# Soft mixture of experts on one core: 21 result tiles at fixed places in turn, instead of at the next free place of a shared pool

## The chip, the cores and the metric

The kernel runs on one core of one Trainium2 chip. The metric is the device time of one execution in microseconds (us). The kernel before takes 1521.05 us, the median of 3 runs (1519.95 to 1521.68).

A core has a matrix engine (PE, with PEld for its weight loads), a vector engine (DVE), a scalar engine (ACT), a GpSimd engine (POOL) and SyncE (SP). In this kernel SP and POOL do almost nothing but issue DMA transfers. Every engine runs its own list of instructions strictly in the order of that list; a wait at the head of a list holds up all that stands behind it.

## The reference

Every token gets all eight experts, weighted by a softmax over its router logits:

```python
probs = softmax(router_logits)                  # 16 x 512 x 8
output = 0                                      # 16 x 512 x 2048
for e in range(8):
    output += probs[:, :, e:e+1] * (x @ expert_weights[e])   # 512 -> 2048
```

Written as one product this is Z times W: Z has 8192 rows (tokens) and 8 x 512 columns (x scaled by each expert's probability), W has 8 x 512 rows and 2048 columns.

## The kernel before

The product is done in a seven-product (Strassen-Winograd) scheme. On the outer level, tokens come in pairs of row blocks of 256, the experts in two groups of four, and the output columns in two halves of 1024. Four of the seven outer products (called 1, 5, 2 and 4) are computed in four stages by `sub_product`, which applies the same scheme once more inside. Their results go to DRAM, to the buffers `kept1`, `kept5`, `kept2` and `kept4`, in tiles of 128 tokens x 512 columns of float32 (256 KB). The remaining three outer products (6, 7 and 3) are computed in the last stage, the loop over `q` at line 432, here called the main stage, and are added there to the kept ones.

`sub_product` (lines 284 to 339) runs over row blocks; for each of two sets of 128 tokens (`u`) it does seven products of 8 matmuls and fills eight result tiles: four copies of a PSUM bank made by ACT (`keep`, line 316) and four sums made by DVE (`put`, line 321), which SP stores to DRAM (`to_kept`).

The main stage has 16 values of `q`, two of `u` and two of `n`: 64 turns, each a column half of 512 columns for one row block pair. Here a turn is called a half and numbered from 0. A half needs four loads by SP of kept products (`from_kept`, line 279), in the order m1, m5, m4, m2, and does this:

1. ACT copies m1 into a PSUM bank (line 461).
2. DVE adds m2 to m1 in m2's tile (line 462, called the m2 sum), and POOL stores it to the output. This needs no result of PE.
3. PE adds 16 matmuls (operand s2) to that bank; DVE adds m5 (line 465, the first sum, into m1's tile).
4. PE adds 16 more (s3) to the same bank, and can begin only when the first sum has read it. DVE makes two sums, into m5's and m4's tiles (lines 467 and 469), and POOL stores both.
5. PE does 16 matmuls (s4) in another bank; DVE adds it to m1's tile (line 471, the last sum), and POOL stores it.

Ahead of this DVE makes the operands a11, s2, s3, s4 for each `u` by four multiplications (`mul`) and three subtractions from xT and pT tiles, which SP loads; there are 8 such tiles (`xpool`).

The order of each engine's list and the place of each tile in SBUF are worked out when the program is built, by a planner that walks the program with costs of its own for each instruction and takes, for each engine, the earliest instruction in program order that it believes to be ready. On the chip the lists and places are fixed, and semaphores hold an instruction until its data and its place are really free.

All result tiles of `sub_product`, all loads of kept products, and the small tiles of the softmax and the identity come from one pool, `hpool`, under one name with 21 places of 2 KB per partition. In the program as built, tiles take these places strictly in program order, each the place that the planner believes to have been free longest. So no load of the main stage gets a place before the last result tile of the fourth stage has got one. In the middle of the main stage m1 and m2 get the place of the tile 26 back, m5 of that 29 back, and m4 of that 3 back, which is m2 of the half before, since m2 is given up early.

The lines that matter below: `softmax` at 152, `early_p` at 195, `early_z` at 202, `half` at 273, `from_kept` at 279, `sub_product` at 284, and the main stage at 432 to 472. L88 is the one line at which every DVE addition, subtraction or multiplication is recorded, L99 that of SP's DMAs, L102 that of POOL's loads, L108 that of the matmuls.

Of the kernel before, what the change touches and what calls it, by code (L numbers as in the profile page):

```python
# [19 lines left out]


# [1 line left out]

# [8 lines left out]
def kernel(  # L32
# [8 lines left out]
    P = 128  # L41
    f16 = mybir.dt.float16
    f32 = mybir.dt.float32
# [4 lines left out]
    E, _, EH = expert_weights.shape  # L48
    T = B * S
    C = H // P  # L50
    HE = E // 2
    NB = 512
# [11 lines left out]
    zpool = ctx.enter_context(tc.tile_pool(name="zpool", bufs=12))  # L64
    xpool = ctx.enter_context(tc.tile_pool(name="xpool", bufs=8))
    spool = ctx.enter_context(tc.tile_pool(name="spool", bufs=5))
    hpool = ctx.enter_context(tc.tile_pool(name="hpool", bufs=21))

# [7 lines left out]

    K8 = 2 * C
    BLOCKS = ((0, 0), (1, 0), (0, 1), (1, 1))  # L80

    last = {}

    def note(i):
        last[i.ins.engine] = i.ins

    def tt(o, a, b, op):
        note(nc.vector.tensor_tensor(out=o, in0=a, in1=b, op=op))  # L88

    @contextmanager  # L90
    def behind():

        with ExitStack() as stack:
            for i in list(last.values()):
                stack.enter_context(tc.issue_after(i))
            yield

    def sp(o, i):
        note(nc.sync.dma_start(out=o, in_=i))  # L99
# [4 lines left out]
    def bank():  # L104
        return psum.tile([P, NB], f32, name="ps", tag="ps")

    def mm(ps, z, w, start, stop):
        nc.tensor.matmul(ps, z, w, start=start, stop=stop, skip_group_check=True)  # L108
# [5 lines left out]
    def new_w():  # L114
        return wpool.tile([P, K8, NB], f16, name="w", tag="w")

    def cast_w(q, kn, e, t):
        k, n = kn
        pool(t[:, ds(e * C, C), :],
             expert_weights[(q // 10 - 1) * HE + 2 * k + e, :,  # L120
                            ds((q % 10 - 1) * NH + n * NB, NB)].rearrange("(c p) n -> p c n", p=P))

    def load(what, kn, gate=True):
        t = new_w()
        if gate:
            note(nc.vector.memset(t.rearrange("p (e c) n -> p e c n", e=2)[:, :, 0, 0:2], 0.0))  # L126
        if (what, kn) in stored:
            pool(t, stored[what, kn])
        else:
            for e in range(2):  # L130
                cast_w(what, kn, e, t)
        return t
# [17 lines left out]


    def softmax(lg, J):
        mx = hpool.tile([P, J], f32, name="mx", tag="h")
        nc.vector.tensor_reduce(out=mx, in_=lg, axis=AX, op=mybir.AluOpType.max)
        tt(lg, lg, mx.unsqueeze(2).to_broadcast([P, J, E]), SUB)
        nc.scalar.activation(out=lg, in_=lg, func=mybir.ActivationFunctionType.Exp)  # L156
        sm = hpool.tile([P, J], f32, name="sm", tag="h")
        nc.vector.tensor_reduce(out=sm, in_=lg, axis=AX, op=ADD)
        nc.vector.reciprocal(out=sm, in_=sm)
        pf = hpool.tile([P, E, J], f32, name="pf", tag="h")  # L160
        tt(pf, lg.rearrange("p j e -> p e j"), sm.unsqueeze(1).to_broadcast([P, E, J]), MUL)
        return pf

# [4 lines left out]
    def cast_x(row):  # L168
        xs = spool.tile([P, H], f16, name="xs", tag="xs")
        pool(xs, x_f[ds(row, P), :])  # L170
        return xs
# [2 lines left out]
    early = [2 * HQ * (j // 2) + P * (j % 2) for j in range(NF)]  # L174
    lg0 = []
    for t in range(2):
        lg0.append(hpool.tile([P, 4, E], f32, name="lg0", tag="h"))
        for j in range(0, 4, 2):
            sp(lg0[t][:, ds(j, 2)], lg_f[ds(early[4 * t + j], 2 * P), :].rearrange("(j p) e -> p j e", p=P))
    xs0 = [cast_x(row) for row in early[:2]]  # L180
    ident = hpool.tile([P, P], f16, name="ident", tag="h")
    nc.vector.memset(ident, 1.0)
    nc.gpsimd.affine_select(out=ident, in_=ident, compare_op=mybir.AluOpType.is_equal, fill=0.0, base=0,
                            pattern=[[-1, P]], channel_multiplier=1)
    xs0 += [cast_x(row) for row in early[2:4]]
    b11 = {kn: new_w() for kn in BLOCKS}
    with behind():
        for kn in BLOCKS[:3]:
            for e in range(2):
                cast_w(11, kn, e, b11[kn])  # L190
    xs0 += [cast_x(row) for row in early[4:]]
    for e in range(2):
        cast_w(11, BLOCKS[3], e, b11[BLOCKS[3]])

    def early_p(t):
        pf = softmax(lg0[t], 4)
        ph = hpool.tile([P, HE, 4], f16, name="ph0", tag="h")
        note(nc.vector.tensor_copy(ph, pf[:, 0:HE]))
        return ph
    ph0 = [early_p(0)]  # L200

    def early_z(j, dest):

        diag = hpool.tile([P, HE, P], f16, name="diag", tag="h")
        tt(diag, ident.unsqueeze(1).to_broadcast([P, HE, P]),
           ph0[j // 4][:, :, ds(j % 4, 1)].to_broadcast([P, HE, P]), MUL)
        for c in range(C):
            ps = bank()
            mm(ps, xs0[j][:, ds(c * P, P)], diag.rearrange("p e t -> p (e t)"), True, True)
            src = ps.rearrange("p (e t) -> p e t", e=HE)  # L210
            for i, o in enumerate(dest(c)):
                note((nc.scalar.copy if c % 2 else nc.vector.tensor_copy)(  # L212
                    o, src if o.shape[1] == HE else src[:, ds(2 * i, 2)]))

    z0 = []
    for j in range(4):
        z = zpool.tile([P, HE, C, P], f16, name="z", tag="z")
        early_z(j, lambda c: [z[:, :, c, :]])
        z0.append(z.rearrange("p e c t -> p (e c) t"))
    ph0.append(early_p(1))  # L220
    z1 = [[zpool.tile([P, 2, C, HQ], f16, name="z", tag="z") for k in range(2)] for t in range(2)]


    R = 4
    J = HQ // R
    p_dram = dram.tile([NHQ, 3 * HE, HQ], f16, name="p_dram")
    lg_v = lg_f.rearrange("(h r j) e -> r h j e", r=R, j=J)
    lg = hpool.tile([P, J, E], f32, name="lg", tag="h")
    for r in range(R):
        sp(lg[ds(r * NHQ, NHQ)], lg_v[r])  # L230
    pf = softmax(lg, J)
    ph = hpool.tile([P, 3 * HE, J], f16, name="ph", tag="h")
    nc.scalar.copy(ph[:, 0:HE], pf[:, HE:E])
    nc.scalar.copy(ph[:, HE:2 * HE], pf[:, 0:HE])
    tt(ph[:, 2 * HE:], pf[:, 0:HE], pf[:, HE:E], ADD)
# [35 lines left out]
    kept = {r: [dram.tile([2, HQ, NB], f32, name=f"kept{r}_{i}") for i in range(NI)] for r in (1, 2, 4, 5)}  # L271

    def half():
        return hpool.tile([P, NB], f32, name="h", tag="h")

    def to_kept(r, i, u, n, t):
        sp(kept[r][i][n, ds(u * P, P), :], t)
# [1 line left out]
    def from_kept(r, i, u, n):  # L279
        t = half()  # L280
        sp(t, kept[r][i][n, ds(u * P, P), :])
        return t

    def sub_product(r, odd, first, w, prep, start=0, zs=None):

        for d in range(start, NI // 2):
# [19 lines left out]
            for u in range(HQ // P):  # L306
                banks = {}

                def prod(p, b, start=True):
                    if start:  # L310
                        banks[b] = bank()
                    for k in range(K8):
                        mm(banks[b], z[p][:, k, ds(u * P, P)], w[p][:, k, :], start and k == 0, k == K8 - 1)
                    return banks[b]

                def keep(ps):
                    t = half()
                    nc.scalar.copy(t, ps)  # L318
                    return t

                def put(t, n, a, b, op):
                    o = half()
                    tt(o, a, b, op)
                    to_kept(r, 2 * d + t, u, n, o)

                r1 = keep(prod(1, "x"))
                put(0, 0, prod(2, "b"), r1, ADD)
                r5 = keep(prod(5, "q"))
                r2 = keep(prod(6, "x", False))
                put(0, 1, prod(3, "q", False), r2, ADD)  # L330
                prod(7, "x", False)
                r3 = keep(banks["x"])
                put(1, 1, banks["x"], r5, ADD)
                put(1, 0, r3, prod(4, "d"), SUB)
# [16 lines left out]
    for n in range(2):  # L351
        ps = [bank() for _ in range(4)]
        for k in range(2):
            for e in range(2):
                for j in range(4):
                    for c in range(C):
                        mm(ps[j], z0[j][:, (2 * k + e) * C + c, :], b11[k, n][:, e * C + c, :],
                           k + e + c == 0, k + e == 2 and c == C - 1)
        for j in range(4):
            o = half()  # L360
            nc.scalar.copy(o, ps[j])  # L361
            to_kept(1, j // 2, j % 2, n, o)
        for j in range(2 * n, 2 * n + 2):
            early_z(4 + j, lambda c: [z1[j // 2][k][:, :, c, ds(j % 2 * P, P)] for k in range(2)])
        if n == 0:
            with behind():
                w = finish(inner_weights(b11, new_w()))


    def weights_of_t1():  # L370
        b = {}
        for i, kn in enumerate(BLOCKS):
            b[kn] = load(12, kn)
# [9 lines left out]
    def weights_of_21():  # L383
        b = {}
        yield
        for kn in BLOCKS:
            b[kn] = load(21, kn)
# [7 lines left out]
    def weights_of_t4():  # L395
        b = {}
        for i, kn in enumerate(BLOCKS):
            t, t2 = load(22, kn), load("t1", kn)
# [103 lines left out]
```

## Time and profile before

| | |
|---|---|
| median of 3 runs | 1521.05 us |
| the profiled execution | 1525.74 us |
| its span, first to last instruction | 1524.0 us |
| PE busy | 1468.5 us, 6712 matmuls |
| DVE busy | 1006.9 us |
| ACT busy | 199.9 us |
| mean granted PE clock | 0.990 |
| DMA | 344.60 MB, mean 226 GB/s |

The profiled execution takes 4.7 us more than the median of the runs. The four stages end at about 794 us of the span and the main stage takes the rest. The page's second part shows the span in 40 slices of 38.1 us, in tenths; before the last slice PE dips only in the 21st to 24th, and its clock only in the 22nd, at the change from the fourth stage to the main one.

### The profile page before, as it was taken

The page shows a single profiled execution, that of the slowest core. Times are in us where ns is not written, and L with a number is a line of the kernel's source. Part 1 is how long each engine was busy: PE and PEld are TensorE (multiplying, and loading weights), DVE is VectorE, ACT ScalarE, POOL GpSimd, SP SyncE. Part 2 cuts the span into 40 slices and gives each one's busy share as a digit, 9 for nine tenths or more (in the row PEclk, how much of TensorE's full clock was granted, in tenths as well). Part 3 has the DMA queues.
Part 4 walks back from the last instruction along what each step waited for, and adds up shares of the span by engine and source line. Part 5 has one row for each costly group of instructions (what it writes and reads, how often), then busy time and mean ns, then how long its engine had stood idle before and what let it go on. Part 6 is the DMA issues. An engine that isn't in the chain of part 4 may idle for free.

```text
span 1524.0 us, 18110 instructions
## 1 busy us (share of the span) xinstructions
PE 1468.5 (96%) x6712; PEld 658.3 (43%) x6712; DVE 1006.9 (66%) x1148; ACT 199.9 (13%) x350; POOL 220.2 (14%) x397
## 2 busy tenths in 40 slices
PE   9999999999999999999987889999999999999997
PEld 3444444444444444444433334444444444444443
DVE  6866776566867868667575656676667666766622
ACT  3211111111111121111110000000000000000000
POOL 3201101110001000010001111212211121212111
PEclk9999999999999999999998999999999999999999
DMA  9999967999579954699659766777777676777521
GB/s 163 236 221 256 238 166 180 235 273 236 170 240 346 345 194 134 180 266 296 250 212 394 232 205 228 239 229 239 230 240 219 227 226 229 232 243 228 201 104 62
DMA packets 200920, 344.60 MB, mean 226 GB/s; under 512 B 55808, under 2 KB 85504, under 8 KB 195200
## 3 DMA queue, kind: packets, MB, share of 16 engines
q1 hardware_dynamic: 145408, 220.75, 47.1%
q0 software_dynamic: 55424, 122.71, 28.8%
q8 instruction: 52, 0.85, 0.2%
q14 instruction: 36, 0.29, 0.1%
HBM read 201.62 MB, written 163.77 MB: 240 GB/s over the span
## 4 chain that ended last, share of the span: by engine, by line
PE 52%; issue 37%; POOL 9%; DMA 2%; POOLq 0%; DVE 0%; ACT 0%; SPq 0%; ACTq 0%; DVEq 0%
PE ps L108 52%; POOL out_dram L457 9%; DMA h<-kept 1%; DMA pT<-p_dram 1%; POOLq L457 0%; DMA lg<-in_router_logits_dram 0%; DVE h L88 0%; DVE z L88 0%; ACT L156 0%; SPq L99 0%; DVE diag L88 0%; ACT ps L461 0%; POOLq L497 0%; ACT lg L156 0%; DVE pf L88 0%
## 5 line engine op out<-in xcount | busy, mean ns | idle before, releaser
L108 PE MATMUL ps<-w,z 128*128 128x512 f16 x6672 | 1455.6, 380 | 42.1 <-DVE h L88 26.3
L108 PEld LDWEIGHTS <-z 128*128 128x128 f16 x6672 | 653.5, 98 | 843.6 <-issue 66.9
L88 DVE TENSOR_TENSOR h<-ps,h 128x512 f32<-128x512 f32 x442 | 298.0, 687 | 321.3 <-PE ps L108 207.5
L88 DVE TENSOR_TENSOR z<-xT,pT 128x2048 f16<-128x2048 f16 x248 | 299.2, 1218 | 21.5 <-PE ps L108 12.2
L88 DVE TENSOR_TENSOR z<-z 128x2048 f16<-128x2048 f16 x220 | 268.5, 1222 | 34.6 <-PE ps L108 25.3
L318 ACT COPY h<-ps 128x512 f32<-128x512 f32 x248 | 145.4, 586 | 601.8 <-PE ps L108 591.8
L457 POOL DMA_DIRECT2D out_dram<-h x256 | 138.4, 541 | 582.5 <-DVE h L88 567.1
L461 ACT COPY ps<-h 128x512 f32<-128x512 f32 x64 | 37.7, 590 | 640.9 <-DVE h L88 607.4
L88 DVE TENSOR_TENSOR h<-h 128x512 f32<-128x512 f32 x64 | 44.2, 690 | 96.4 <-DMA h<-kept 88.0
L102 POOL DMA_DIRECT2D xs<-in_x_dram x72 | 38.6, 539 | 304.3 <-DMA xT<-xs 296.8
L88 DVE TENSOR_TENSOR w<-w 128x4096 f16<-128x4096 f16 x32 | 73.0, 2286 | 4.8 <-PE ps L108 3.1
L88 DVE TENSOR_TENSOR h<-h,ps 128x512 f32<-128x512 f32 x62 | 42.3, 682 | 11.7 <-PE ps L108 11.7
L102 POOL DMA_DIRECT2D w<-in_expert_weights_dram x40 | 30.0, 761 | 134.5 <-DVE w L126 85.8
L102 POOL DMA_DIRECT2D w<-wd x12 | 6.5, 539 | 242.2 <-DVE w L126 135.1
L212 DVE CAST z<-ps 128x256 f16<-128x256 f32 (+1 forms) x24 | 10.7, 506 | 8.8 <-PE ps L108 8.8
L108 PE MATMUL ps<-diag,xs 128*128 128x512 f16 x32 | 10.2, 483 | 2.5 <-DVE diag L88 2.5
L102 POOL DMA_DIRECT2D w<-wdt x12 | 6.5, 546 | 32.0 <-DVE w L88 17.8
L212 ACT CAST z<-ps 128x256 f16<-128x256 f32 (+1 forms) x24 | 9.2, 479 | 4.3 <-PE ps L108 4.2
L108 PEld LDWEIGHTS <-xs 128*128 128x128 f16 x32 | 3.7, 118 | 9.1 <-issue 7.2
L361 ACT COPY h<-ps 128x512 f32<-128x512 f32 x8 | 4.7, 585 | 15.7 <-PE ps L108 15.7
L88 DVE TENSOR_TENSOR diag<-ident,ph 128x512 f16<-128x512 f16 x8 | 5.2, 685 | 0.1
L76 PE MATMUL every<-zero 128*128 128x512 f16 x8 | 3.6, 631 | 1.3 <-DVE zero L73 1.3
(20 smaller groups left out, 13.1 us busy)
## 6 DMA issues: line engine op xcount, KB each, us to landing
kept<-h SPq DMA_DIRECT2D x256, 256.0 KB, 4.8
h<-kept SPq DMA_DIRECT2D x256, 256.0 KB, 3.4
out_dram<-h POOLq DMA_DIRECT2D x256, 256.0 KB, 3.7
pT<-p_dram SPq DMA_DIRECT2D x124, 256.0 KB, 4.8
w<-in_expert_weights_dram POOLq DMA_DIRECT2D x40, 512.0 KB, 12.9
xT<-x SPq DMA_DIRECT2D x60, 256.0 KB, 4.2
wdt<-w SPq DMA_DIRECT2D x12, 1024.0 KB, 8.5
w<-wdt POOLq DMA_DIRECT2D x12, 1024.0 KB, 14.0
```

The source lines that it names most:

```text
L76: nc.tensor.matmul(every[:, i, :], zero[:, 0:P], zero, start=True, stop=True)
L88: note(nc.vector.tensor_tensor(out=o, in0=a, in1=b, op=op))
L102: note(nc.gpsimd.dma_start(out=o, in_=i))
L108: nc.tensor.matmul(ps, z, w, start=start, stop=stop, skip_group_check=True)
L212: note((nc.scalar.copy if c % 2 else nc.vector.tensor_copy)(o, src if o.shape[1] == HE else src[:, ds(2 * i, 2)]))
L318: nc.scalar.copy(t, ps)
L361: nc.scalar.copy(o, ps[j])
L457: nc.gpsimd.dma_start(out=out_f[ds((2 * q + odd) * HQ + u * P, P), ds(cols * NH + n * NB, NB)], in_=t)
L461: nc.scalar.copy(ps, m1)
```

## The change

The pool of 21 shared places becomes 21 names of one place each, h0 to h20. A counter hands the names out in the order in which the program asks for tiles, so a tile always takes the place of the tile asked for 21 before it, whatever the planner believes to be free. Five small tiles that live long or come early (two logit tiles, the identity, two probability tiles) leave the pool for places of their own in a second pool, `cpool`.

```diff
+from itertools import count
...
-    hpool = ctx.enter_context(tc.tile_pool(name="hpool", bufs=21))
+    hpool = ctx.enter_context(tc.tile_pool(name="hpool", bufs=1))
+    cpool = ctx.enter_context(tc.tile_pool(name="cpool", bufs=1))
...
+    turn = count()
+
+    def h_tile(shape, dtype):
+
+        return hpool.tile(shape, dtype, name="h", tag=f"h{next(turn) % 21}")
...
-        mx = hpool.tile([P, J], f32, name="mx", tag="h")
+        mx = h_tile([P, J], f32)
...
-        sm = hpool.tile([P, J], f32, name="sm", tag="h")
+        sm = h_tile([P, J], f32)
...
-        pf = hpool.tile([P, E, J], f32, name="pf", tag="h")
+        pf = h_tile([P, E, J], f32)
...
-        lg0.append(hpool.tile([P, 4, E], f32, name="lg0", tag="h"))
+        lg0.append(cpool.tile([P, 4, E], f32, name=f"lg0_{t}"))
...
-    ident = hpool.tile([P, P], f16, name="ident", tag="h")
+    ident = cpool.tile([P, P], f16, name="ident")
...
-        ph = hpool.tile([P, HE, 4], f16, name="ph0", tag="h")
+        ph = cpool.tile([P, HE, 4], f16, name=f"ph0_{t}")
...
-        diag = hpool.tile([P, HE, P], f16, name="diag", tag="h")
+        diag = h_tile([P, HE, P], f16)
...
-    lg = hpool.tile([P, J, E], f32, name="lg", tag="h")
+    lg = h_tile([P, J, E], f32)
...
-    ph = hpool.tile([P, 3 * HE, J], f16, name="ph", tag="h")
+    ph = h_tile([P, 3 * HE, J], f16)
...
     def half():
-        return hpool.tile([P, NB], f32, name="h", tag="h")
+        return h_tile([P, NB], f32)
```

No instruction is added or removed, and no transfer: only places, the waits that follow from them, and the order that the planner makes of them can differ.

## The prediction

> **What bounds the kernel now.** I read the page first: which engine is full, and where it is not.
>
> ```profile
> span 1524.0 us, 18110 instructions
> PE 1468.5 (96%) x6712; PEld 658.3 (43%) x6712; DVE 1006.9 (66%) x1148; ACT 199.9 (13%) x350; POOL 220.2 (14%) x397
> ...
> PEclk9999999999999999999998999999999999999999
> ```
>
> PE is the bound. Started back to back, matmuls lie 216 ns apart in the trace, so 6712 need 1448 us of the 1524.0; 76 us is all that any change of waits can touch. To see where they lie I cut the span by stage (columns: stretch, its length, then busy time and count of PE, PEld, DVE, ACT, POOL, the granted clock, DMA share, GB/s).
>
> ```profile
> 600.00:780.00 180.00, 180.00 (x835) 81.58 (x834) 125.64 (x138) 34.60 (x59) 10.81 (x17) 1.00 0.75 230
> 794.00:811.00 17.00, 1.55 (x7) 0.55 (x5) 12.10 (x12) 0.59 (x1) 0.53 (x1) 0.62 1.02 420
> 811.00:890.00 79.00, 67.09 (x284) 28.83 (x283) 44.25 (x54) 4.95 (x9) 14.59 (x27) 0.93 0.81 276
> 890.00:1450.00 560.00, 547.01 (x2501) 244.16 (x2500) 378.94 (x442) 31.02 (x53) 112.96 (x209) 1.00 0.70 228
> ```
>
> The count in brackets is the better measure: count times 0.216 us against the length. 835 take 180.4 of 180: the four stages lose nothing. The change of stage loses 17 - 7 x 0.216 = 15.5 us, the next 79 us lose 79 - 284 x 0.216 = 17.7, the 560 us after that 560 - 2501 x 0.216 = 19.8.
>
> Then the timeline at the change of stage, for who is late (start, length, engine, line; in brackets the idle time before and what ended it).
>
> ```profile
> 794.14 1.23 DVE L88 TENSOR_TENSOR z<-xT,pT 128x2048 f16<-128x2048 f16 x1 [3.73 <-DMA pT<-p_dram]
> ...
> 796.41 0.38 SPq L99 DMA_DIRECT2D h<-kept  x1
> ...
> 809.70 0.59 ACT L461 COPY ps<-h 128x512 f32<-128x512 f32 x1 [16.56 <-DMA h<-kept]
> 810.34 1.86 PE L108 MATMUL ps<-w,z 128*128 128x512 f16 x4 [15.45 <-ACT ps L461]
> ```
>
> PE waits for the first m1, which SP issues only at 796.41, after PE is out of work, and which lands 13.2 us later, since the DMA engines are full (share 1.02). Last, a turn of the main stage, and what SP waits for there.
>
> ```profile
> 1003.70 0.69 DVE L88 TENSOR_TENSOR h<-h 128x512 f32<-128x512 f32 x1 [2.43 <-DMA h<-kept]
> ...
> 1006.71 1.88 DVE L88 TENSOR_TENSOR h<-ps,h 128x512 f32<-128x512 f32 x3
> ...
> 1014.83 0.69 DVE L88 TENSOR_TENSOR h<-h 128x512 f32<-128x512 f32 x1 [3.50 <-DMA h<-kept]
> 1015.43 1.22 DVE L88 TENSOR_TENSOR z<-xT,pT 128x2048 f16<-128x2048 f16 x1
> ```
>
> ```profile
> SPq L99 <- DMA out_dram<-h: 445.4, 227, 6.7
> ```
>
> The m2 sum at 1014.83 belongs to a half five to six turns ahead of PE; nobody needs it yet. But DVE's list is fixed, so it stands idle 3.50 us and what PE needs comes late: PE's gap after 1021.96 waits 1.56 us for a first sum. SP waits for stores of the output to land, to have places again.
>
> **The change part by part.** No instruction, byte or DMA is added or removed; priced are places.
>
> *The five small tiles and the stages.* lg0, ident and ph0 leave the turn: the main row of 21 is whole from the start. In the four stages places were already 20 to 23 tiles apart in the program as built; now 21. A set of eight tiles lasts 12.1 us of PE (56 matmuls), so a place comes back after 2.6 sets, 32 us; its use (copy or sum 0.6 us, store 4.8 us to landing by the page) is far below. Cost nothing; the cover is 25 us.
>
> *The change of stage.* Today the first load stands in SP's list behind the stage's last sum but two (stored at 796.00). With its own name, m1 of half 0 waits only for the tile 21 back, the fourth of the last set but two, which a sum gives up 27 us before the end at 794.4; m2 waits for a store of 770.9 and its landing. So half 0 loads between 768 and 780, half 1 by about 785 (its last place is free after a sum at 781.1), halves 2 and 3 by some 795. In the stretch from 760 to 784 the DMA engines move only 108 GB/s, so there is room. Gone: the 15.6 us gap, and the slow matmuls after it, 12 at 427 instead of 216 ns, 2.5 us: together 18.1.
>
> The 17.7 us to 890 are three gaps of 3.4, 4.5 and 4.5 us (from 837.5, 851.6 and 878.4), some fifteen slow matmuls (3.2 us), and small ones. In them DVE's m2 sums wait for loads that queue up at over 390 GB/s, by up to 7.3 us. With 3 to 4 MB of loads moved ahead the burst is thinner; but the list is again one planned with prompt loads. Ends 0 and 15.8 us gone; I take 9, just over half, as one of three waits has pT loads in it, which do not move.
>
> What is late next: at 794.14 DVE waits for a pT issued at 785.55, not for a kept load, and has 8.7 us of work until 802.7 that it then does late. PE's first sum of half 0 is due at about 797.8 (16 matmuls); s4 matmuls cover 1 to 3 us. A new gap of 0 to 9 us; I take 3. Below that end lies nothing, since the work exists already. The seven 1 MB weight loads issue between 784.2 and 794.5 and land in 9 to 14.5 us; the last pair is first needed some 18 us into the stage, at 812, and should just be there.
>
> A rule to weigh: 12 slow matmuls here took 5.1 us at a granted clock of 0.5 after 15.6 us of idling. The Trainium skill, page "TensorE: Matmul & The Clock Gate", section on the HAM clock gate, says that the array falls to half clock after an idle window of about 3.4 us and recovers after about 3.4 us of work. By the page a remaining gap under 3.4 us costs no slow matmuls, one over it 8 of them, an estimate of 1.7 us. The sum above has 3 us and none; with the rule against it, it is 1.7 us worse.
>
> *The middle of the main stage.* Now every place is 21 back: m1 follows m2 of six halves before, m5 the m1, m4 the m5 and m2 the m4 of five halves before. m4 no longer waits for the store of the half before. But the m2 sum of half j+5 now hangs on the second of the two sums after s3 of half j (it was the first, for j+6). Cost of that circle: from 1006.71 (first of the two) to 1014.83 (the m2 sum that its place was for) 8.1 us; then the m2 sum 0.6, one operand step 1.2, and the same sum again at 1016.57: 9.9 us around, against 48 x 0.216 = 10.4 us of PE; with a second step between 11.0 (1016.57 to 1027.55). So the circle is about as long as PE's turn today, and that makes the 19.8 us. In the new one the second sum adds 0.6. But the m2 sum becomes ready later in the plan too, so that an operand step (1.2) may stand ahead of it. Ends: loss 0 (20 gained) and 0.6 us for each of some 60 halves on top of what exists (36 lost). I take 0, between them, as the two shifts cancel.
>
> Sum: -18.1 - 9 + 3 + 0 = -24. The profiled execution of 1525.74 would become 1501.6; the median lies 4.7 lower, 1521.05 - 24 = 1497.
>
> A second rule: the Trainium skill, "DMA: Bandwidth & Descriptors", section "Issuing engines are not separate DMA queues", says that all queues share the same 16 engines and interleave. This speaks against the change: the early loads can push back the weights. The trace's 420 GB/s at share 1.02 agrees that there is a ceiling. By the rule each MB that lands within the weights' 27 us instead of after them costs an estimate of 2.4 us, so 1 to 2 MB cost 2 to 5 us beyond the cover of 4; the sum would be 0 to 1 us worse.
>
> **The rivals.**
>
> *Faster still* (17%): the new circle is shorter than PE's turn. Then most of the 19.8 us go too: 1477. For it: 9.9 fits under 10.4. Against: the one of 11.0 does not.
>
> *No change* (9%): the gap only changes its owner. pT at 794.14, weights and early sums keep PE waiting as long, and the middle is a little worse: 1518 to 1524. For it: DMA is full from 784 on whatever comes first. Against: 108 GB/s before that.
>
> *Slower* (19%): the circle closes over the last sum of a half. If SP's list has m2 behind m5, whose place hangs on the last sum of half j, then around it goes 8.1 us, two issues of 0.32, and four sums of 0.6, 11.1 us, plus the operand steps between: one of 1.2 makes 12.3 instead of the present 10.8 (43.1 us from gap to gap over four halves). Over 60 halves +1.5 us each: 90, less the 24, 1587; with no step between, 18 less 24, 1515. It decides from 0.4 us a half on, when it eats the 24. For it: places given in program order today. Against: pT loads do overtake h loads in SP's list, so a load that has its place need not stay behind one that has not.
>
> **How the numbers follow.** The forecast has 55%, its own range 1478 to 1515 (the ends 0 and 15.8, 0 and 9, and the middle from -12 to +12). A difference under 0.2%, 3 us, is no change for this measurement. Faster: 55 + 17 + 3 from the slow rival's lower end = 75%. Within 0.2%: two thirds of the no-change case, 6%. Slower: the other 16 of the slow rival and 3 of the no-change case, 19%. The range leaves out the upper two thirds of the slow rival and a little of the fast one: 1468 to 1530.
>
> **What would show it.** Right: the first m1 issued before 785 and PE without a gap over 4 us between 790 and 815; a clock of 1.00 there; the four stages as before. For the middle: matmuls in 560 us of it, 2501 now; more is the fast rival, under 2400 the slow one. Wrong would be: SP's waits for output stores longer, DVE idle before m2 sums more than 63 us, or gaps in the fourth stage, where DVE's early m2 sums now stand ahead of its last results.

## The result, and where the time went

The changed kernel takes 1546.82 us, the median of 4 runs (1542.85 to 1551.03), against 1521.37 us for the kernel before (4 runs, 1519.95 to 1523.64): 1.0166 times as long, with a 95% interval of 1.0134 to 1.0199. The forecast was 1497, the range 1468 to 1530. The change makes the kernel 1.7% slower, where it was forecast to make it 1.6% faster.

The profiled execution of the changed kernel took 1544.84 us, 19.1 more than that of the kernel before. The medians lie 25.5 us apart; the 19.1 of the two profiled executions are what can be taken apart below. In the page PE has the same 6712 matmuls and the same busy time, and the span is longer (the 54 more instructions are waits on semaphores).

```profile
span 1543.1 us, 18164 instructions
PE 1468.6 (95%) x6712; PEld 658.4 (43%) x6712; DVE 1004.0 (65%) x1148; ACT 199.4 (13%) x350; POOL 220.1 (14%) x397
...
PEclk9999999999999999999997999999999999999999
```

The same stretches of the span as before the change (stretch, its length, busy time and count of PE, PEld, DVE, ACT, POOL, granted clock, DMA share, GB/s):

```profile
600.00:780.00 180.00, 180.00 (x836) 81.61 (x834) 127.05 (x140) 34.55 (x59) 10.81 (x17) 1.00 0.75 233
794.00:811.00 17.00, 8.69 (x41) 3.82 (x39) 3.56 (x4) 1.67 (x3) 1.58 (x3) 0.90 1.01 412
811.00:890.00 79.00, 59.60 (x251) 25.63 (x251) 54.27 (x61) 3.54 (x6) 12.42 (x23) 0.85 0.74 254
890.00:1450.00 560.00, 531.20 (x2421) 236.67 (x2419) 367.48 (x430) 30.08 (x51) 109.69 (x203) 1.00 0.67 222
```

The fourth stage still loses nothing (836 matmuls in 180 us). But the whole of it comes later, so the stretches cut the main stage at other places. To compare the kernels I cut at matmuls instead: the lost time of a part is the time from its first matmul to the first of the next part, less 0.2157 us for each matmul in it. All sums below go by this; q counts the 16 passes of the main stage's outer loop, of 192 matmuls each.

| part | before | after | difference |
|---|---|---|---|
| steady run of the four stages begins at | 17.1 us | 20.6 us | +3.5 |
| lost in the four stages | 0.5 | 0.5 | 0 |
| lost in q = 0 (change of stage) | 27.6 | 29.1 | +1.5 |
| lost in q = 1 | 6.6 | 4.8 | -1.8 |
| lost in q = 2 to 15 (the middle and the end) | 23.3 | 39.2 | +15.9 |
| sum | | | +19.1 |

**The start.** The timeline of the kernel before, first DVE operations and the first real matmuls (start, length, engine, line):

```profile
6.54 1.90 DVE L88 TENSOR_TENSOR diag<-ident,ph 128x512 f16<-128x512 f16 x3
...
7.38 4.85 PE L108 MATMUL ps<-diag,xs 128*128 128x512 f16 x11 [2.53 <-DVE diag L88]
```

and that of the changed kernel:

```profile
9.47 0.69 DVE L162 TENSOR_REDUCE h<-h 128x64 f32<-128x512 f32 x1 [1.78 <-DMA h<-in_router_logits_dram]
10.19 0.69 DVE L96 TENSOR_TENSOR h<-h 128x512 f32<-128x512 f32 x1
10.80 1.89 DVE L96 TENSOR_TENSOR h<-ident,ph 128x512 f16<-128x512 f16 x3
...
11.63 4.57 PE L116 MATMUL ps<-h,xs 128*128 128x512 f16 x11 [6.77 <-DVE h L96]
```

The 128x512 maximum and subtraction at 9.47 and 10.19 are the softmax of the main logits, which is needed only much later. It now stands in DVE's list ahead of the diagonal tiles on which PE's first products wait, and it waits itself for its load. In the kernel before, one name had 21 places, and tiles took them in program order; that kept the later softmax behind the diagonal tiles. With 21 names there is no such order between the names, and the planner puts it first: in the programs as built, none of the 784 tiles of the pool is taken out of program order before, and 230 of 779 are after.

**The change of stage.** From the timeline of the changed kernel:

```profile
771.94 2.10 SPq L107 DMA_DIRECT2D h<-kept  x2
...
788.06 0.44 SPq L107 DMA_DIRECT2D h<-kept  x1
...
789.67 13.10 SPq L107 DMA_DIRECT2D h<-kept  x4
...
793.06 0.60 ACT L469 COPY ps<-h 128x512 f32<-128x512 f32 x1
...
796.30 0.53 POOL L110 DMA_DIRECT2D w<-wd  x1 [1.20 <-PE ps L116]
...
799.46 0.69 DVE L96 TENSOR_TENSOR h<-h 128x512 f32<-128x512 f32 x1 [10.84 <-DMA h<-kept]
...
811.97 0.69 DVE L96 TENSOR_TENSOR h<-h 128x512 f32<-128x512 f32 x1 [8.95 <-DMA h<-kept]
...
817.55 2.36 DVE L96 TENSOR_TENSOR z<-xT,pT 128x2048 f16<-128x2048 f16 x2 [2.01 <-DMA pT<-p_dram]
...
824.43 0.68 DVE L96 TENSOR_TENSOR h<-ps,h 128x512 f32<-128x512 f32 x1
825.03 0.68 DVE L96 TENSOR_TENSOR h<-h 128x512 f32<-128x512 f32 x1
825.17 5.07 PE L116 MATMUL ps<-w,z 128*128 128x512 f16 x16 [22.48 <-DVE h L96]
```

The early loads did come: m1 of half 0 is issued at 771.94 and copied at 793.06, before PE needs it. Yet PE now stands for 22.48 us (22.9 from the start of one matmul to that of the next, the measure of a gap below), against 15.45 (15.8) before. It waits for the first sum of half 0, at 824.43, which could have run at about 801, when its 16 matmuls were through. What stands ahead of it in DVE's list are the m2 sums of half 1 (799.46, after 10.84 us of idling) and half 2 (811.97, after 8.95), operand steps of q = 1 that wait for pT (817.55), and the last results of the fourth stage. The two m2 loads were issued at 788.06 and, the third of the four from 789.67, at 796.30, and took 11.4 and 15.7 us to the sum that waited for them; seven weight loads of 1 MB were issued between 787.66 and 798.02 (the POOL line at 796.30 is one of them), and the DMA engines were full (share 1.01 in the stretch 794 to 811). The burst also holds up the issue of the loads: by the program as built, the second of these m2 takes the place of a result tile of the fourth stage, whose store was issued at 787.58 and landed at 796.23, after 8.7 us; the next load, m1 of half 3, waits in the same way for a store of 788.59 that landed at 802.44, after 13.9 us.

**The middle.** In the 560 us from 890 on PE does 2421 matmuls, 2501 before. What the engines wait for in that stretch (us in total, times, longest), in the kernel before:

```profile
DVE h L88 <- DMA h<-kept: 62.8, 34, 3.5
...
PE ps L108 <- DVE h L88: 12.7, 12, 1.6
```

and in the changed one:

```profile
DVE h L96 <- DMA h<-kept: 129.0, 50, 5.1
...
PE ps L116 <- DVE h L96: 28.6, 17, 3.1
```

DVE waits twice as long for kept products, and PE twice as long for DVE. Over the whole span SP waits longer for stores of the output to land:

```profile
SPq L107 <- DMA out_dram<-h: 492.7, 213, 7.9
```

The circle that the prediction described can be followed in a turn of the changed kernel:

```profile
1000.67 1.29 DVE L96 TENSOR_TENSOR h<-ps,h 128x512 f32<-128x512 f32 x2 [0.47 <-PE ps L116]
...
1004.24 1.47 SPq L107 DMA_DIRECT2D h<-kept  x2
...
1010.33 0.69 DVE L96 TENSOR_TENSOR h<-h 128x512 f32<-128x512 f32 x1 [2.39 <-DMA h<-kept]
...
1013.33 1.88 DVE L96 TENSOR_TENSOR h<-ps,h 128x512 f32<-128x512 f32 x3
...
1023.38 0.69 DVE L96 TENSOR_TENSOR h<-h 128x512 f32<-128x512 f32 x1 [4.25 <-DMA h<-kept]
1023.99 1.28 DVE L96 TENSOR_TENSOR h<-ps,h 128x512 f32<-128x512 f32 x2
```

The second of the two sums after s3 begins at 1001.27. By the places and lists of the program as built, its tile is stored, the m2 of the half five later is loaded into its place, and the m2 sum of that half runs at 1010.33: 9.1 us. Two operand steps follow, and the next second sum begins at 1013.93: 12.7 us around. The next time around, to 1024.59, takes 10.7 us. PE's turn is 48 x 0.216 = 10.4 us, so both are too long, one of them by 2.3 us.

### The profile page after: what moved, and what is told of

Its sections match the earlier page's. It is cut to its first block, busy times and chain, and to the rows that moved or that the text cites. A ratio compares the mean times of both kernels' runs of the same rounds, so it can differ in the third digit from the quotient of the medians.

```text
span 1543.1 us, 18164 instructions
## 1 busy us (share of the span) xinstructions
PE 1468.6 (95%) x6712; PEld 658.4 (43%) x6712; DVE 1004.0 (65%) x1148; ACT 199.4 (13%) x350; POOL 220.1 (14%) x397
## 4 chain that ended last, share of the span: by engine, by line
PE 51%; issue 35%; POOL 8%; DMA 4%; DVE 1%; SPq 0%; POOLq 0%; DVEq 0%
PE ps L116 51%; POOL out_dram L465 8%; DMA h<-kept 2%; DMA out_dram<-h 1%; DMA pT<-p_dram 1%; DVE h L96 1%; DVE z L96 1%; SPq L107 0%; DMA h<-in_router_logits_dram 0%; POOLq L465 0%; DVE h L162 0%; POOLq L505 0%; DVEq L96 0%; DVEq L162 0%
## 5 line engine op out<-in xcount | busy, mean ns | idle before, releaser
L96 DVE TENSOR_TENSOR z<-xT,pT 128x2048 f16<-128x2048 f16 x248 | 299.0, 1218 | 14.5 <-PE ps L116 12.0
L96 DVE TENSOR_TENSOR h<-h 128x512 f32<-128x512 f32 (+1 forms) x67 | 46.5, 694 | 168.3 <-DMA h<-kept 166.1
L220 DVE CAST z<-ps 128x256 f16<-128x256 f32 (+1 forms) x24 | 10.5, 505 | 12.3 <-PE ps L116 12.3
L116 PE MATMUL ps<-h,xs 128*128 128x512 f16 x32 | 9.4, 454 | 6.8 <-DVE h L96 6.8
L116 PEld LDWEIGHTS <-xs 128*128 128x128 f16 x32 | 3.5, 112 | 12.8 <-issue 10.4
L96 DVE TENSOR_TENSOR h<-ident,ph 128x512 f16<-128x512 f16 x8 | 5.2, 677 | 0.0
(22 smaller groups left out, 10.9 us busy)
## 6 DMA issues: line engine op xcount, KB each, us to landing
w<-in_expert_weights_dram POOLq DMA_DIRECT2D x40, 512.0 KB, 13.1
```

The lines of the kernel that those rows point to most:

```text
L220: note((nc.scalar.copy if c % 2 else nc.vector.tensor_copy)(o, src if o.shape[1] == HE else src[:, ds(2 * i, 2)]))
```

## The experiments

My theory after reading this: places and loads do what the diff says, and the loss comes from DVE's list. An m2 sum is issued as soon as its load is believed to be there, five halves ahead of PE, and DVE idles before it while the sums PE waits for stand behind it; giving each tile a fixed place makes that wait longer. The start is a loss of its own, from the order of requests. Rivals: the five small tiles do something; the DMA engines alone are the cause at the change of stage; the circle over the last sum of a half, the slow rival of the prediction, is what acts in the middle.

Batches ran on different chips; each ratio is to the kernel before on the same chip (1527.65, 1529.67 and 1527.5 us there). Where an expectation gives a time, it is the ratio that it should be compared by: the kernel before ran 6 to 8 us longer on these chips than on the first. "Lost" is counted as in the table above.

### The small tiles alone

The kernel before, with only the five small tiles moved to places of their own:

```diff
+    cpool = ctx.enter_context(tc.tile_pool(name="cpool", bufs=1))
...
-        lg0.append(hpool.tile([P, 4, E], f32, name="lg0", tag="h"))
+        lg0.append(cpool.tile([P, 4, E], f32, name=f"lg0_{t}"))
...
-    ident = hpool.tile([P, P], f16, name="ident", tag="h")
+    ident = cpool.tile([P, P], f16, name="ident")
...
-        ph = hpool.tile([P, HE, 4], f16, name="ph0", tag="h")
+        ph = cpool.tile([P, HE, 4], f16, name=f"ph0_{t}")
```

> Only the five small tiles leave the pool; its 21 shared places stay. Theory (what was lost is the program order of requests, which 21 names give up): requests stay in order, so the first product of the start begins at 7.4 us as before, and the time is 1518 to 1525. Rival (the small tiles' own places change the start): it begins at 11.6 as after the change, and 3 to 5 us are lost, 1525 to 1527.

Measured: 1528.51 us, ratio 1.0002 (0.9985 to 1.0018). The first real product begins at 7.16 us, the middle loses 27.8 us. The small tiles cost nothing, and the start is not theirs. That PE begins 4 us later in the changed kernel comes from the 21 names.

### The order of the start given back

The changed kernel, with the two later softmaxes put behind what stands before them in program order (`behind()` is the kernel's own helper for that):

```diff
-    ph0.append(early_p(1))
+    with behind():
+        ph0.append(early_p(1))
...
-    pf = softmax(lg, J)
+    with behind():
+        pf = softmax(lg, J)
```

> The changed kernel with the second and third softmax put behind what the program issues before them on each engine. Theory: the start begins at 7.4 us instead of 11.6, and the 3.5 us lost there come back, with the rest as after the change: 1541 to 1545. Rival (the start is late for its places or its loads): begins at 11.6, 1547.

Measured: 1550.44 us, ratio 1.0147 (1.0124 to 1.0171). The first real product begins at 7.16 us instead of 11.63, the steady run at 15.4 instead of 20.6, and the stages after it lose nothing, as before. So 5 us of the start are the order, and they are part of what the change costs (the first profile of the kernel before, with 17.1, reached full clock at 13.1 us, that with only the small tiles moved at 11.2, with a steady run from 15.7). The ratio came down by only 0.2%, with intervals that overlap, and the middle lost 52.4 us in this profile against 39.2 in the first. The lists of DVE and SP are the same in the two programs there, yet the middle's loss differs by 13.2 us between two chips, or two executions. Of these, 5.9 lie in matmuls at half clock (five stretches of 3.4 us at granted clock 0.5 from q = 2 on, one in the first profile), the rest in longer gaps; why the gaps are longer is open.

### The m2 sums held back: with the turn, and with the shared pool

Each m2 sum is put behind the last sum of the half before it in DVE's list. Nothing else is touched: loads may still run ahead. Once in the changed kernel, once in the kernel before:

```diff
+    tail = [None]
...
-                    tt(o, a, b, op)
+                    tail[0] = tt(o, a, b, op)
...
-                tt(m2, m1, m2, ADD)
+                with tc.issue_after(tail[0]):
+                    tt(m2, m1, m2, ADD)
...
-                tt(m1, prod(s4, w3, n), m1, ADD)
+                tail[0] = tt(m1, prod(s4, w3, n), m1, ADD)
```

With the turn:

> The changed kernel with each m2 sum put behind the last sum of the half before on DVE (for the first half, behind the last sum of the fourth stage). Theory (DVE's early m2 sums wait for loads and hold up the sums that PE needs): DVE's waits for kept loads fall from 160 us to under 25, the gap of 22.9 us at the change of stage to under 8, the loss for each q from 3 us to under 1: 1480 to 1500. Rival (places at 21 tiles' distance are too few, SP's loads come late): m2's place is now given up even later, so loads come no earlier, 1545 to 1570.

With the shared pool:

> The kernel before, with 21 shared places, and the same hold on the m2 sums. Theory: the middle gains as with the turn (about 20 us to 1450), but the first load of the main stage still stands behind the last request of the fourth stage, so a gap of 12 to 18 us stays there: 1495 to 1510. Rival (places): the pool loses its early places, 1521 or more.

Measured with the turn: 1506.41 us, ratio 0.9859 (0.9833 to 0.9885); with the shared pool 1497.49, ratio 0.9797 (0.977 to 0.9823). The stretch from 890 on of the first,

```profile
890.00:1450.00 560.00, 560.00 (x2562) 250.03 (x2561) 380.98 (x448) 31.26 (x53) 115.63 (x214) 1.00 0.72 233
```

and of the second:

```profile
890.00:1450.00 560.00, 560.00 (x2562) 250.12 (x2560) 375.38 (x443) 31.25 (x53) 115.68 (x215) 1.00 0.73 233
```

Both do 2562 matmuls there, and both lose 8.1 us in q = 2 to 15, 0.58 in each q and 42.0 us from one to the next without exception. No wait of DVE for a kept product is left in that stretch. So all of the middle's loss but these 8.1 us, in both kernels, was DVE standing before an m2 sum that nobody needed yet. The 0.58 us lie at four places in each q where two matmuls start 0.35 to 0.36 us apart; what holds them there was not looked into. Against the kernels without the hold on the same chip (27.8 us in the kernel with the small tiles moved, 52.4 in that with the start given back) the hold is worth 20 us in the middle with the shared pool and 44 with the turn. For the whole execution with the shared pool it is 30 us (1527.65 to 1497.49): q = 0 and 1 lose less as well, 24.2 instead of 33.5.

The change of stage did not come out as expected with the turn: q = 0 still loses 28.2 us.

```profile
794.49 0.94 SPq L110 DMA_DIRECT2D pT<-p_dram  x2
...
817.30 2.36 DVE L97 TENSOR_TENSOR z<-xT,pT 128x2048 f16<-128x2048 f16 x2 [21.16 <-DMA pT<-p_dram]
...
824.38 4.00 PE L119 MATMUL ps<-w,z 128*128 128x512 f16 x9 [21.05 <-DVE h L97]
```

DVE now stands 21.16 us before an operand step of q = 1, first used in half 4, whose pT was issued at 794.49 and landed 22.3 us later. With the m2 sums out of the way, the next early consumer in the list took their place.

### The weight loads left out

To see what the traffic does, six of the seven late weight loads are left out: the second column half of the main stage uses the weights of the first. Half of the output columns are then computed with the weights of the other half; all other work stays.

```diff
-                    w[k, n] = load(what, (k, n), False)
+                    w[k, n] = load(what, (k, n), False) if n == 0 else w[k, 0]
```

With the turn and the m2 sums held back:

> The turn with the m2 sums held, and six of the seven weight loads at the end of the fourth stage left out: the second column half takes the weights of the first, so that half of the output is not the reference's. Theory (the loads of h and pT land late because 6 MB of weights share the DMA engines): landings of pT at the change of stage fall from 22 us to under 6, and the gap from 21 us to under 4. Rival (SP's list or the places make the loads late): the gap stays above 10.

Measured in one run: 1486.72 us. The gap at the change of stage falls from 21.4 to 5.6 us and q = 0 loses 7.2 us instead of 28.2. The DMAs issued there (between 784 and 824 us of the span; KB each, median us to landing) in the kernel with the weights,

```profile
pT<-p_dram SPq DMA_DIRECT2D x2, 256.0 KB, 22.3
```

and without them:

```profile
pT<-p_dram SPq DMA_DIRECT2D x6, 256.0 KB, 6.2
```

The row without the weights has six loads; the two that stand for those above, issued at 792.17 and 792.88, took 7.3 and 7.2 us, and DVE's list around them is the same. So some 15 of the 22.3 us are the traffic of the weights, as far as one run tells. With the turn alone:

> The changed kernel itself with the same six weight loads left out, with the same part of the output not the reference's. Theory (the m2 sums cost the stage change only because the loads they wait for are slowed by the weights): the gap of 22.9 us falls under 6; the middle stays as after the change, 2 to 5 us lost for each q. Rival (the planner's order alone blocks PE): the gap stays above 12.

Measured in one run: 1537.87 us; the gap falls from 22.9 to 9.0 us, q = 0 loses 13.6, and the middle is as bad as without this edit (49.7 us lost). That is between the two expectations: the weights are the larger part of the gap, but without them DVE's order alone still leaves 9 us. In the kernel before:

> The kernel before with six of the seven weight loads at the end of the fourth stage left out, so that half of the output columns are not the reference's. Theory (the 15.8 us gap is mostly the slow landing of the first m1 among the weights): m1 lands in 3 to 5 us instead of 13.2, and the gap falls to 6 to 8 us. Rival (the gap is the late issue alone): it stays above 12.

Measured in one run: 1518.74 us; the first m1 is issued at 793.59, nearly as late as ever, but ACT waits only 3.5 us for it, and the gap falls from 15.8 to 2.8. That is less than expected: even in the kernel before, the late issue costs most of the gap only because the weights share the DMA engines with the load. Not all of the change of stage goes with it: q = 0 and 1 still lose 14.7 and 8.5 us.

### The operand steps held back as well

The changed kernel with the start's order, the m2 sums held back, and the operand steps of q = 1 put behind the last sums of half 0 (for u = 0) and half 1 (for u = 1):

```diff
+            with (tc.issue_after(sums[u]) if q == 1 else nullcontext()):
-            a11 = mul(xa, p1a, 0, HE, u * P, P)
+                a11 = mul(xa, p1a, 0, HE, u * P, P)
...
+                sums.append(tail[0])
```

> The changed kernel with the start and the m2 sums held as in the two runs before, and the operand steps of q = 1 put behind the last sum of half 0 (first set of tokens) and of half 1 (second set). Theory (with m2 sums held, the gap at the change of stage is DVE waiting in a step for a pT that is needed 40 us later): the gap of 21 us falls under 6 and the slow matmuls go with it: 20 to 26 us less than the turn with the hold, and 3.5 for the start: 1478 to 1488 where the kernel before takes 1521. Rival (the weights themselves come late, whatever DVE does): PE waits for the weight loads in place of DVE, a gap of 10 us or more stays.

Measured: 1493.59 us, ratio 0.9763 (0.9748 to 0.9777). q = 0 loses 16.8 us. The large gap is gone; what is left are two of 1.6 and 3.3 us at 808 to 810 and one of 8.5 at 835, where the steps of q = 2 now stand before their pT. Holding those too:

```diff
-            with (tc.issue_after(sums[u]) if q == 1 else nullcontext()):
+            with (tc.issue_after(sums[4 * q - 4 + u]) if q in (1, 2) else nullcontext()):
```

> The changed kernel with start and m2 sums held, and the operand steps of q = 1 and q = 2 each put behind the last sum four halves ahead of their use. Theory (the gap of 8.5 us that stayed at 835 us is DVE waiting in the steps of q = 2 for a pT): it goes, the stage change costs 6 to 11 us in place of 16.8, and the ratio to the kernel before is 0.968 to 0.974. Rival (the weights are late): the gap moves to PE's waits for weight loads, ratio 0.976 or more.

Measured: 1484.91 us against 1527.5, ratio 0.9718 (0.9688 to 0.9749), the fastest of all, and faster than the kernel before and the changed one. The change of stage in it:

```profile
794.00:811.00 17.00, 14.68 (x67) 6.44 (x66) 4.63 (x7) 0.59 (x1) 2.72 (x5) 1.00 1.01 398
811.00:890.00 79.00, 73.14 (x326) 32.25 (x326) 60.97 (x70) 4.72 (x8) 14.59 (x27) 0.96 0.85 272
```

67 matmuls in the first 17 us instead of 7 before the change and 41 with it. q = 0 loses 10.0 us, and among the largest gaps left is one before the weights themselves and one in which DVE waits 7.53 us for a pT, with a sum behind the steps that need it (the store named at 816.34 is not it: PE goes on as the sum of 815.61 ends):

```profile
811.57 0.38 PE L119 MATMUL ps<-w,z 128*128 128x512 f16 x1 [2.05 <-DMA w<-wd]
...
813.33 2.36 DVE L97 TENSOR_TENSOR z<-xT,pT 128x2048 f16<-128x2048 f16 x2 [7.53 <-DMA pT<-p_dram]
...
815.61 0.68 DVE L97 TENSOR_TENSOR h<-ps,h 128x512 f32<-128x512 f32 x1
...
816.34 14.03 PE L119 MATMUL ps<-w,z 128*128 128x512 f16 x55 [4.40 <-DMA out_dram<-h]
```

The same two edits, of the m2 sums and of the steps, in the kernel before, whose start needs none:

```diff
-            a11 = mul(xa, p1a, 0, HE, u * P, P)
+            with (tc.issue_after(sums[4 * q - 4 + u]) if q in (1, 2) else nullcontext()):
+                a11 = mul(xa, p1a, 0, HE, u * P, P)
...
-                tt(m2, m1, m2, ADD)
+                with tc.issue_after(tail[0]):
+                    tt(m2, m1, m2, ADD)
```

> The kernel before, with 21 shared places, the m2 sums held and the operand steps of q = 1 and q = 2 held in the same way. It tells what the early places of the turn are worth once DVE's list no longer waits. Theory: the first m1 still stands behind the last request of the fourth stage and lands late, so the stage change costs 16 to 24 us, 8 to 13 more than with the turn: ratio 0.976 to 0.983. Rival (places do not matter there either): the same ratio as with the turn within 0.002.

Measured: 1498.58 us, ratio 0.981 (0.9783 to 0.9837), no better than with the m2 sums alone. There the first m1 is late again:

```profile
809.88 0.59 ACT L466 COPY ps<-h 128x512 f32<-128x512 f32 x1 [18.00 <-DMA h<-kept]
810.52 34.66 PE L111 MATMUL ps<-w,z 128*128 128x512 f16 x151 [16.89 <-ACT ps L466]
```

Here the change does what it says: between the two kernels with the same lists held back, the places in turn and the loads that run ahead in them are worth 13.7 us (1498.58 to 1484.91). Of the 10.5 between the two profiles, 10.4 lie in q = 0 and 1 (19.1 and 2.8 against 10.0 and 1.5 us lost); the middle is alike (8.0 in both).

### The circle over the last sum

The slow rival said that the circle closes over the last sum of a half if SP's list has m2 behind m5. In the changed kernel as built SP's order is m4, m2, m5, and m1 of a later half, so it does not. Two kernels make it close there. The first puts SP's loads of kept products in program order:

```diff
         t = half()
-        sp(t, kept[r][i][n, ds(u * P, P), :])
+        with (tc.issue_after(queue[-1]) if queue else nullcontext()):
+            i = nc.sync.dma_start(out=t, in_=kept[r][i][n, ds(u * P, P), :])
+        note(i)
+        queue.append(i.ins)
```

> The changed kernel with SP's loads of kept products in program order (m1, m5, m4, m2), so that the load of m2 stands behind that of m5, whose place hangs on the last sum of a half. The change itself has them out of that order. Theory (the circle from a sum by its store, the load and the m2 sum back to that sum sets the middle): the circle now closes over the last sum, a q takes 46 to 50 us in place of 44.4, as with 20 names: 1570 to 1620. Rival (SP's order has no part in it): 1542 to 1556.

Measured: 1610.79 us, ratio 1.0542 (1.0514 to 1.057); a q of the middle takes 44.3 to 52.7 us, 49.5 in the mean, 12.4 a half. The prediction's working for this rival had 12.3 a half with one operand step in the circle, and 1587 us for the whole; that counted on the 24 us of the change of stage, and without them it is 1611. That 1610.79 is so near is luck, since the chip was slower: by the ratio it is 1604, and the middle lost 82.6 us more than in the first profile of the kernel before, where the rival had 90. The second has 20 names instead of 21, so that m1 takes the place of an earlier m1, which the last sum gives up:

```diff
-        return hpool.tile(shape, dtype, name="h", tag=f"h{next(turn) % 21}")
+        return hpool.tile(shape, dtype, name="h", tag=f"h{next(turn) % 20}")
```

> The changed kernel with 20 names in turn instead of 21, so that each of m1, m5, m4, m2 takes the place of its own kind five halves back. Theory (the middle is set by the circle from a sum by its store, the load that takes its place, and the m2 sum back to that sum): m2's sum needs m1, whose place is now held until the last sum of a half instead of until the early m2 store, so the circle closes over the last sum; a q of the middle goes from 44.4 us to 46 to 50: 1570 to 1620. Rival (the circle is not what binds; one place more or less in 21): the same as after the change within 5 us, 1542 to 1552.

Measured: 1594.72 us, ratio 1.0419 (1.0388 to 1.0449); 48.2 us for a q of the middle, 12.1 a half. What DVE waits for from 890 on in it:

```profile
DVE h L96 <- DMA h<-kept: 157.1, 47, 7.4
...
PE ps L116 <- DVE h L96: 56.1, 24, 5.5
```

Both agree with a middle that is set by the length of this circle when nothing holds the m2 sums: over the last sum 12.1 to 12.4 us a half, over the second of the two sums after s3 (the changed kernel) 11.1 to 11.4, over the first of the two (the kernel before) 10.8 to 10.9, without it 10.5.

## Why the prediction was wrong

**The small tiles and the stages: nothing.** The stages lose nothing, as said, and the small tiles cost nothing. But the start was not looked at. The prediction said that only places, waits and the planner's order could differ, and then priced only the order of the main stage. The order of requests of one name was a part of the kernel before that the change removed: 3.5 us in the two profiles, 5 by the experiment.

**The change of stage: -18.1, -9, +3.** The first step was right that m1 would be issued early (771.9, between the 768 and 780 forecast) and wrong in what that is worth: the gap did not go. The term that failed is the "new gap of 0 to 9 us; I take 3": it is 22.9, since what PE waits for is not m1 but the first sum, and that stands in DVE's list behind m2 sums and operand steps whose data come late. The step counted how long the late work is (8.7 us); what counts is the idling ahead of it, 10.84 and 8.95 us. It also had halves 2 and 3 loaded by some 795, and the weights landing in 9 to 14.5 us. In the profile of the kernel before they took 5.1 to 15.9 us, and after the change the stores whose places the loads need took 8.7 and 13.9 us, so that m2 of half 2 was issued at 796.30 and m1 of half 3 at 802.46. For q = 0 and 1 together it forecast -24 and got -0.3. The rival that the gap "only changes its owner", given 9%, is what happened here, with its reason too: the DMA engines are busy whatever comes first (share 0.86 from 784 to 794, 1.01 from there to 811).

The Trainium skill's rule in "DMA: Bandwidth & Descriptors", section "Issuing engines are not separate DMA queues", that transfers share the same 16 engines whichever engine starts them, was weighed at "0 to 1 us worse", by the time that early loads take from the weights. The runs agree with the rule and show its effect the other way round: the weights take time from the small loads, 22.3 us for a 256 KB pT against 7.2 without six of the weight loads.

**The clock.** The gap was priced at no slow matmuls if under 3.4 us, from the section on the HAM clock gate in "TensorE: Matmul & The Clock Gate" of the Trainium skill, which puts half clock behind an idle window of about 3.4 us. The gap at 872.64 was 2.7 us long, and from 875.9 on PE ran 3.4 us at half clock:

```profile
875.90:879.30 3.40, 3.40 (x10) 1.18 (x8) 0.93 (x2) 0.00 (x0) 0.00 (x0) 0.50 0.90 292
```

Here the measurement decides: a gap well under 3.4 us can be followed by half clock. Nor does its length alone tell, for gaps of 3.0 us at 983.93 and 3.3 us at 1341.65 were not followed by it. In this trace all changes of the clock lie on one grid of 3.41 us, and between 850 and 1500 us half clock came after those intervals of the grid, and only those, in which PE stood for more than some 2.1 us: 2.5 in the one that ends at 875.93, 2.1 in the one that ends at 1077.31. The grid splits the two longer gaps into 1.0 and 1.8 us and into 1.7 and 1.4.

**The middle: 0, between -20 and +36.** The mechanism was right: the m2 sum hangs on the second sum of five halves before, SP waits longer for the stores (425.9 us in the 560 from 890 on, 406.2 before), DVE waits longer before m2 sums. The size was off: 15.9 us in the profiles, and 24.6 between the two kernels of the second chip that differ by it (27.8 and 52.4 us lost), 0.28 to 0.44 us for each of 56 halves where the step had 0 with an end of 0.6. That "the two shifts cancel" was an assumption with no row behind it. The row that the prediction itself showed, a circle of 9.9 and one of 11.0 us against a turn of 10.4, had no room left, and lengthening it could only cost.

**The rivals.** The slow one, at 19%, had the right sign and the wrong circle; in the kernel as built its condition does not hold. Where it was made to hold, the price came out at 12.4 and 12.1 us a half, against its 12.3. A fourth case was missing: the circle over the second sum with no compensation, and the gap of the change of stage staying.

**What would show it.** DVE's idling before m2 sums in that stretch, 62.8 us before, is 129.0; SP waits 492.7 us for stores of the output instead of 445.4; and "DVE's early m2 sums now stand ahead of its last results", which run at 814.85 to 820.43, 16 to 18 us later than before (795.28 to 798.75) if the 3.5 us of the start are taken off; the gap that comes of it lies in half 0 and not in the fourth stage. The prediction named the first two, and gaps in the fourth stage for the third, as signs that it is wrong, and gave them no price. Of the signs for it, the first m1 came before 785 and the four stages are as before; the gap over 4 us and a clock of 0.90 between 794 and 811 speak against it. The matmul count from 890 on, 2421, lies between that of the forecast and the 2400 of the slow rival.

## What to carry to other kernels

A transfer that runs ahead helps only if its consumer does not stand early in an in-order list: an engine that waits for data needed five turns later delays what is needed now, and an earlier transfer does not help until the consumer is held back; here holding it was worth 20 us of the middle with the old places and 44 with the new, and only when the operand steps were held too were the early loads worth their 14. When a gap ends on a transfer, look first at what else is in flight at that moment, since issuing the transfer earlier or removing the traffic are different cures. And a pool whose places are requested under one name also fixes an order of the work; splitting the name gives that order up, everywhere it was relied on.

## What was not expected of the hardware

A load of 256 KB took 22.3 us from issue to landing while seven loads of 1 MB were in flight, 11.4 and 15.7 us for two others, and 7.2 with six of the seven left out; the DMA engines moved 412 GB/s between 794 and 811. Half clock followed a gap of PE of 2.7 us and not one of 3.3, by how the gaps lie on the grid of 3.41 us on which the clock changes. The same lists lost 39 us in the middle in one profile and 52 in another, and the kernel before took 1521 us on one chip and 1527 to 1530 on others; what makes that difference was not tried.
